# Four-layer hybrid attention network: both pairs of maxima of a step side by side, the second pair in a double bank, and each gated output split once

## The chip, the cores and the metric

The kernel runs on one core of one Trainium2 chip. The metric is the device time of one execution in microseconds (us). The engines are TensorE (PE, matrix products; PEld is its weight load), VectorE (DVE), ScalarE (ACT), GpSimd (POOL) and SyncE (SP, which only issues DMA here). A 128x512 float32 PSUM tile is one bank; PSUM holds eight.

## The reference

```python
for i in range(DEPTH):                       # 4 layers, mixer kinds A, B, C, A
    h  = rms_norm(x,  norm_g[i]) * (1 + sc)  + sh     # 1024 latent tokens, width 1024
    hc = rms_norm(xc, norm_g[i]) * (1 + scc) + shc    # 256 context tokens
    u, z = split(h @ w_in)                   # mixer columns and the gate
    o = mixer(u, uc, ...)                    # A: softmax(q k / 8) v, 16 heads, 4 kv heads
    x  = x  + gt  * ((o  * silu(z))  @ w_out)
    xc = xc + gtc * ((oc * silu(zc)) @ w_out)         # not in the last layer
return x
```

`sh`, `sc`, `gt` come from a product of the conditioning vector with `ada_w`. Mixer A attends from every token to context and latent keys; B within a window of 8 x 16; C takes the difference of two softmaxes.

## The kernel before, in words

Every product is done on float32 operands split in two parts, a rounded one (`hi`, made by `round_pool` on POOL, L130) and the rest (`lo`, by `sub` on DVE, L133); a product is three matmuls. The layers follow one another: projection of the norm's result, the z (gate) projection, attention, output projection.

**Attention A** (layers 0 and 3) works in units: a pair of heads by 512 queries, with ten key tiles in layer 0's latent part. `unit_events` gives each piece of a unit a time on a scale of steps and sorts them; one step holds two key tiles. In a step PE does the scores of two key tiles (`st`, L700 and L701, eight matmuls into two tiles from the pool `pa`, two buffers of two banks each), which ACT turns into exponentials (L705); the product of an earlier step's exponentials with the values (`o`, L725, eight matmuls, "PV"); and, for a unit ahead, two pairs of products (`sl` L653, `sc` L668) for the maximum over the keys, in single banks from the pool `pb` (four buffers). Each of these banks is reduced by one TENSOR_REDUCE on DVE (L660, L674). The times of the two pairs within a step are the table `SLOTS` (L781); scores stand at 0.05 and 0.15, PV at 0.4 and 0.45. The maxima of a unit become a row (`rows`: transpose `mT` L686, copy on ACT `mr` L688, a DMA), which takes part in the scores. The exponentials are summed on POOL and, for the last two key tiles, on DVE (L739), then `mixed` (L745, L747), a row sum on PE (L753) and the division. Only PE's order is pinned to the table's order; the other engines take theirs from the scheduler.

**out_proj** (from L872) runs over `work`, first all token tiles with the first half of the output columns (h=0), then all with the second (h=1): ten tiles, eight in the last layer. `start(i)` splits the gated output of the next tile into `ogt` hi and lo in two slots (four roundings on POOL, four subtractions on DVE); `products` makes 24 matmuls `y` (L897); DVE scales by the gate (`yg`, L934), POOL adds the residual (`xo`, L935). In h=1, except in the last layer, the tile's norm for the next layer follows: square sum, `rstd` on POOL, `xn` on DVE (L285), and one tile later eight transposes on PE (`xT`, L293) and the modulation (`hs`, ACT L314 and DVE L305; `hhi` L130, `hlo` L133). The slots come from one pool of 42 buffers of 128x1024 (`WHOLES`), which also holds the gated outputs, the probabilities and weights.

Of the kernel before, what the change touches and what calls it, by code (L numbers as in the profile page):

```python
# [15 lines left out]
ALU = mybir.AluOpType  # L16
AX = mybir.AxisListType
# [3 lines left out]
P = 128  # L21
D = 1024
KT = D // P
# [49 lines left out]
class Net:  # L73
# [554 lines left out]
    def softmax_unit(self, qscr, heads, Ks, vsrc, og, pair, t0, n, kts, finish):  # L628
# [19 lines left out]
        def max_lat(qt, c):  # L648

            for hh in range(2):  # L650
                k, q = high(hh, 0)
                ps = self.pb("sl")
                nc.tensor.matmul(  # L653
                    ps, q[:, qt * P : (qt + 1) * P], k[:, c * 512 : c * 512 + 512], start=True, stop=True,
                    tile_position=(hh * HD, 0),
                )
                st["ps", hh] = ps
            for hh in range(2):
                o = st["M"][:, hh * nq + qt, c : c + 1]
                nc.vector.tensor_reduce(out=o, in_=st["ps", hh], axis=AX.X, op=ALU.max)  # L660

        def max_ctx(a):
            ps = [self.pb("sc").rearrange("p (q k) -> p q k", k=CTX) for _ in range(2)]
            for i in range(2):
                qt = a * 2 + i
                for hh in range(2):
                    k, q = high(hh, 1)
                    nc.tensor.matmul(  # L668
                        ps[hh][:, i, :], q[:, qt * P : (qt + 1) * P], k, start=True, stop=True,
                        tile_position=(hh * HD, 0),  # L670
                    )
            for hh in range(2):
                o = st["M"][:, hh * nq + a * 2 : hh * nq + a * 2 + 2, 2 if lat else 0]
                nc.vector.tensor_reduce(out=o, in_=ps[hh], axis=AX.X, op=ALU.max)  # L674
# [34 lines left out]
        u.maxima = [lambda q=q, c=c: max_lat(q, c) for q in range(nq) for c in range(2) if lat]  # L709
        u.maxima += [lambda a=a: max_ctx(a) for a in range(nq // 2)]  # L710
# [70 lines left out]
    SLOTS = (0.25, 0.8)  # L781

    def unit_events(self, units, extra=()):
# [10 lines left out]
        for u, g in reversed(list(zip(units, starts))):  # L794
            if c >= g - self.LEAD:
                c, i = g - self.LEAD - 1, len(self.SLOTS) - 1
            for m in reversed(u.maxima):
                ev.append((c + self.SLOTS[i], m))
                c, i = (c, i - 1) if i else (c - 1, len(self.SLOTS) - 1)
# [61 lines left out]
    def out_proj(self, l, wop, steps, og, tiles):  # L861
# [46 lines left out]
        def start(i):  # L908
            ot = parts()
            split(work[i][1], range(4), ot)  # L910
            halves[i] = ot

        start(0)
        for i, (h, t) in enumerate(work):
# [9 lines left out]
            products(ps, h, halves.pop(i), range(KT))  # L924
# [793 lines left out]
```

## Time and profile before

| what | value |
|---|---|
| runs | 3665.51, 3666.45, 3667.39 us; median 3666.45 |
| profiled execution, its own time | 3671.03 us |
| its span; mean granted clock | 3669.2 us; 0.983 |
| PE / PEld busy | 3518.5 us (96%) / 2615.8 us (71%) |
| DVE / POOL / ACT busy | 2153.7 (59%) / 1998.8 (54%) / 1323.0 us (36%) |
| attention A, layer 0 (354 to 860 us) | PE 487.69 of 506, DVE 293.56, ACT 222.10, POOL 331.94 |
| attention A, layer 3 (3156 to 3560 us) | PE 399.26 of 404, DVE 253.78, ACT 187.45, POOL 308.20 |
| output projection, layer 0, h=0 (860 to 925 us) | PE 63.40 of 65 |
| splits of the gated output | POOL 304 x 0.57 us, DVE 304 x 0.56 us (173.3 and 170.8 us) |
| chain that ended last | PE 68%, DVE 16%, POOL 9% of the span |

The stages lie one behind the other, so each is read by itself: the busy time of each engine in its stretch, then what PE's idle time there waited for. In the timelines consecutive instructions of one kind are joined to one row (x8: eight of them), and the bracket tells how long the engine stood before the row and which instruction released it.

### The profile page before, as it was taken

What the parts mean: (1) busy time and instruction counts of PE and PEld (TensorE: products, weight loads), DVE (VectorE), ACT (ScalarE), POOL (GpSimd) and SP (SyncE); (2) the same over time, 40 slices, a digit from 0 to 9 for tenths busy, and PEclk for the clock granted to TensorE, in tenths of its full rate; (3) what the DMA queues carried; (4) which work ended last, traced back from release to release, by engine and by line L of the source; (5) the groups of instructions that cost most, each with busy time, mean ns of one, the idle gap of its engine ahead of it and who ended that gap; (6) DMA issues with size and microseconds to landing.
All of it is one profiled execution on the core that took longest, in us unless ns stands there. A gap on an engine that the chain in (4) does not pass through costs nothing.

```text
span 3669.2 us, 50527 instructions
## 1 busy us (share of the span) xinstructions
PE 3518.5 (96%) x18594; PEld 2615.8 (71%) x18594; DVE 2153.7 (59%) x3675; ACT 1323.0 (36%) x2756; POOL 1998.8 (54%) x2006
## 2 busy tenths in 40 slices
PE   7999999998899999999999999999989999999989
PEld 4887444446788888887778888888877787544447
DVE  5542555565742412888766510899995754566655
ACT  3221444441321212774222211677761221344430
POOL 5540656678631310667765510567776743477786
PEclk9999999999999999999999999999999999999989
DMA  6352543513244444552425432221313334111112
GB/s 208 78 135 83 158 130 103 182 55 97 96 116 138 104 126 111 166 151 69 138 78 137 130 117 61 82 87 38 98 40 99 110 93 125 46 46 37 46 39 86
DMA packets 229459, 370.39 MB, mean 101 GB/s; under 512 B 34088, under 2 KB 124120, under 8 KB 229212
## 3 DMA queue, kind: packets, MB, share of 16 engines
q1 hardware_dynamic: 228636, 367.01, 34.1%
q8 instruction: 148, 2.42, 0.3%
q14 instruction: 99, 0.81, 0.1%
q10 hardware_dynamic: 576, 0.15, 0.0%
HBM read 270.36 MB, written 96.57 MB: 100 GB/s over the span
## 4 chain that ended last, share of the span: by engine, by line
PE 68%; DVE 16%; POOL 9%; issue 4%; DMA 2%; ACT 1%; SPq 0%; POOLq 0%; ACTq 0%; DVEq 0%
PE proj L382 21%; PE zT L467 11%; PE o L725 8%; PE y L897 6%; PE st L700 5%; PE st L701 4%; PE sl L653 3%; DVE ml L1450 3%; PE o L1120 2%; POOL rstd L146 2%; DVE wlo L133 2%; DVE ogt L133 1%; PE qkT L437 1%; POOL hhi L130 1%; POOL p L739 1%
## 5 line engine op out<-in xcount | busy, mean ns | idle before, releaser
L739 POOL TENSOR_TENSOR p<-p,p 128x1024 f32<-128x1024 f32 x224 | 540.1, 2411 | 326.1 <-PE o L725 287.4
L382 PE MATMUL proj<-whi,hhi 128*128 128x512 f32 x1408 | 556.7, 395 | 3.2 <-POOL whi L130 1.9
L382 PE MATMUL proj<-wlo,hhi 128*128 128x512 f32 x1408 | 551.3, 392 | 3.9 <-DVE wlo L133 3.8
L382 PE MATMUL proj<-whi,hlo 128*128 128x512 f32 x1408 | 551.1, 391 | 0.0
L660 DVE TENSOR_REDUCE M<-sl 128x1 f32<-128x512 f32 x512 | 326.8, 685 | 292.5 <-PE sl L653 292.5
L705 ACT ACTIVATE p<-st 128x1024 f32<-128x1024 f32 (+1 forms) x336 | 324.4, 1003 | 314.8 <-PE st L701 303.1
L897 PE MATMUL y<-whi,ogt 128*128 128x512 f32 x1216 | 389.7, 398 | 16.7 <-POOL ogt L130 13.1
L133 DVE TENSOR_TENSOR wlo<-wraw,whi 128x1024 fp32r<-128x1024 f32 x136 | 213.5, 1584 | 217.8 <-POOL whi L130 193.0
L725 PE MATMUL o<-p,v 128*64 128x512 f32 x1344 | 324.5, 605 | 1.7 <-DVE M L660 1.1
L130 POOL TENSOR_SCALAR whi<-wraw 128x1024 fp32r<-128x1024 f32 x136 | 179.0, 1321 | 254.0 <-DMA wraw<-in_c_w_in_dram 91.3
L382 PEld LDWEIGHTS proj<-wlo,hhi 128*128 128x128 f32 x1408 | 265.8, 189 | 58.9 <-DVE wlo L133 6.0
L382 PEld LDWEIGHTS proj<-whi,hhi 128*128 128x128 f32 x1408 | 265.8, 189 | 57.5 <-POOL hhi L130 2.4
L382 PEld LDWEIGHTS proj<-whi,hlo 128*128 128x128 f32 x1408 | 265.6, 189 | 55.4
L897 PEld LDWEIGHTS y<-whi,ogt 128*128 128x128 f32 x1216 | 230.7, 190 | 73.2 <-POOL ogt L130 16.8
L467 PE MATMUL zT<-hhi,whi 128*128 128x512 f32 (+1 forms) x704 | 256.6, 365 | 5.9 <-DVE qklo L133 5.6
L404 ACT ACTIVATE y<-proj 128x1024 f32<-128x1024 f32 (+1 forms) x68 | 65.5, 964 | 527.4 <-PE proj L382 470.0
L467 PE MATMUL zT<-hhi,wlo 128*128 128x512 f32 (+1 forms) x704 | 254.3, 361 | 1.3 <-DVE wlo L133 1.3
L467 PE MATMUL zT<-hlo,whi 128*128 128x512 f32 (+1 forms) x704 | 254.2, 361 | 0.0
L897 PE MATMUL y<-wlo,ogt 128*128 128x512 f32 x608 | 239.6, 394 | 0.0
L146 POOL TENSOR_TENSOR rstd<-rstd,mhalf 128x16 f32<-128x16 f32 (+3 forms) x132 | 230.8, 1748 | 10.9
L700 PE MATMUL st<-q,k 128*128 128x512 f32 x512 | 218.3, 426 | 2.3 <-ACT p L705 2.3
L410 DVE TENSOR_TENSOR y<-y,rstd 128x1024 f32<-128x1024 f32 (+1 forms) x68 | 104.1, 1531 | 193.0 <-POOL rstd L146 193.0
(221 smaller groups left out, 7242.7 us busy)
## 6 DMA issues: line engine op xcount, KB each, us to landing
adaw<-in_ada_w_dram SPq DMA_DIRECT2D x96, 512.0 KB
xo<-xres SPq DMA_DIRECT2D x86, 256.0 KB
wraw<-in_a_w_in_dram SPq DMA_DIRECT2D x40, 512.0 KB
k<-k SPq DMA_DIRECT2D x40, 512.0 KB
q<-qkhi SPq DMA_DIRECT2D x76, 256.0 KB
q<-qklo SPq DMA_DIRECT2D x76, 256.0 KB
q<-q SPq DMA_DIRECT2D x136, 128.0 KB
wraw<-in_b_w_in_dram SPq DMA_DIRECT2D x32, 512.0 KB
```

Source lines behind the costliest of these rows:

```text
L130: self.nc.gpsimd.tensor_scalar(out=out, in0=in_, scalar1=1.0, scalar2=0.0, op0=ALU.mult, op1=ALU.add)
L133: self.nc.vector.tensor_tensor(out, a, b, op=ALU.subtract)
L146: nc.gpsimd.tensor_tensor(r, r, self.mhalf[:, :n], op=ALU.pow)
L382: nc.tensor.matmul(ps[:, i, :], self.h_op(a, 2 * tp + i, k), wop(b, k), start=(k == 0 and j == 0), stop=(k == KT - 1 and j == 2),)
L467: nc.tensor.matmul(ps, wop(a, k)[:, b * P : (b + 1) * P], self.h_cols(c, g, k), start=(k == 0 and j == 0), stop=(k == KT - 1 and j == 2),)
L660: nc.vector.tensor_reduce(out=o, in_=st["ps", hh], axis=AX.X, op=ALU.max)
L700: nc.tensor.matmul(ps[:, hh, :], self.k_op(K, 0, kt), q1[:, hh, :], start=True, stop=False)
L701: nc.tensor.matmul(ps[:, hh, :], self.k_op(K, 1, kt)[0 : HD + 1], q2[:, hh, :], start=False, stop=True)
L705: nc.scalar.activation(p, ps, AF.Exp, scale=HD**-0.5)
L725: nc.tensor.matmul(st["o"][hh * HD : (hh + 1) * HD, :], v(hh, kt), p[:, hh, :], start=j == 0, stop=j == N - 1, tile_position=(0, hh * HD),)
L739: eng.tensor_tensor(a, a, p, op=ALU.add)
L897: nc.tensor.matmul(ps, ot[a][:, k, :], wop[h](b, k), start=(k == 0 and j == 0), stop=(k == KT - 1 and j == 2))
```

## The change

The title given with the change names three things. The diff has lines for two of them; those of the differential layer (L1450, L1451) are the same in both programs.

1. `SLOTS` goes from (0.25, 0.8) to (0.25, 0.3), so the second pair of maxima of a step stands directly behind the first, ahead of PV. The second pair of a step (`i == 1`) goes into one tile of `pa` (two banks) and is reduced by one TENSOR_REDUCE over both (L658 of the changed file); the first stays in two tiles of `pb` (L661).
2. `start` in `out_proj` splits a token tile once, in h=0, and keeps the two slots until h=1 has used them.

```diff
--- before.py
+++ after.py
@@ -645,33 +645,47 @@
             K = st["K"][hh][kt][1 - hh] if kt == 0 else st["K"][hh][1][:, 1 - hh, :]
             return K[rows], st["q"][0][rows, hh, :]
 
-        def max_lat(qt, c):
-
+        def banks(double):
+
+            if double:
+                both = self.pa("sl")
+                return both, [both[:, hh * 512 : hh * 512 + 512] for hh in range(2)]
+            return None, [self.pb("sl") for _ in range(2)]
+
+        def largest(out, both, ps, n):
+
+            if both is not None:
+                nc.vector.tensor_reduce(out=out, in_=both.rearrange("p (h q k) -> p h q k", h=2, q=n), axis=AX.X, op=ALU.max)
+                return
+            for hh in range(2):
+                nc.vector.tensor_reduce(
+                    out=out[:, hh, :], in_=ps[hh].rearrange("p (q k) -> p q k", q=n), axis=AX.X, op=ALU.max
+                )
+
+        def max_lat(double, qt, c):
+
+            both, ps = banks(double)
             for hh in range(2):
                 k, q = high(hh, 0)
-                ps = self.pb("sl")
                 nc.tensor.matmul(
-                    ps, q[:, qt * P : (qt + 1) * P], k[:, c * 512 : c * 512 + 512], start=True, stop=True,
+                    ps[hh], q[:, qt * P : (qt + 1) * P], k[:, c * 512 : c * 512 + 512], start=True, stop=True,
                     tile_position=(hh * HD, 0),
                 )
-                st["ps", hh] = ps
-            for hh in range(2):
-                o = st["M"][:, hh * nq + qt, c : c + 1]
-                nc.vector.tensor_reduce(out=o, in_=st["ps", hh], axis=AX.X, op=ALU.max)
-
-        def max_ctx(a):
-            ps = [self.pb("sc").rearrange("p (q k) -> p q k", k=CTX) for _ in range(2)]
+            M = st["M"][:, : 2 * nq, c].rearrange("p (h q) -> p h q", h=2)
+            largest(M[:, :, qt : qt + 1], both, ps, 1)
+
+        def max_ctx(double, a):
+            both, ps = banks(double)
             for i in range(2):
                 qt = a * 2 + i
                 for hh in range(2):
                     k, q = high(hh, 1)
                     nc.tensor.matmul(
-                        ps[hh][:, i, :], q[:, qt * P : (qt + 1) * P], k, start=True, stop=True,
+                        ps[hh][:, i * CTX : (i + 1) * CTX], q[:, qt * P : (qt + 1) * P], k, start=True, stop=True,
                         tile_position=(hh * HD, 0),
                     )
-            for hh in range(2):
-                o = st["M"][:, hh * nq + a * 2 : hh * nq + a * 2 + 2, 2 if lat else 0]
-                nc.vector.tensor_reduce(out=o, in_=ps[hh], axis=AX.X, op=ALU.max)
+            M = st["M"][:, : 2 * nq, 2 if lat else 0].rearrange("p (h q) -> p h q", h=2)
+            largest(M[:, :, a * 2 : a * 2 + 2], both, ps, 2)
 
         def whole():
             st["mm"] = self.small([P, 32], "mm", 3)[:, : 2 * nq]
@@ -706,8 +720,8 @@
             st["p", j] = p
 
         u.load, u.whole, u.rows = load, whole, rows
-        u.maxima = [lambda q=q, c=c: max_lat(q, c) for q in range(nq) for c in range(2) if lat]
-        u.maxima += [lambda a=a: max_ctx(a) for a in range(nq // 2)]
+        u.maxima = [lambda d, q=q, c=c: max_lat(d, q, c) for q in range(nq) for c in range(2) if lat]
+        u.maxima += [lambda d, a=a: max_ctx(d, a) for a in range(nq // 2)]
         u.scores = [lambda j=j, kt=kt: scores(j, kt) for j, kt in enumerate(kts)]
         u.products, u.ends = finish(st, kts, n, pair, t0, og)
         return u
@@ -778,7 +792,7 @@
         return [lambda j=j, kt=kt: pv(j, kt) for j, kt in enumerate(kts)], ends
 
     LEAD = 2
-    SLOTS = (0.25, 0.8)
+    SLOTS = (0.25, 0.3)
 
     def unit_events(self, units, extra=()):
 
@@ -795,7 +809,7 @@
             if c >= g - self.LEAD:
                 c, i = g - self.LEAD - 1, len(self.SLOTS) - 1
             for m in reversed(u.maxima):
-                ev.append((c + self.SLOTS[i], m))
+                ev.append((c + self.SLOTS[i], lambda m=m, i=i: m(i == 1)))
                 c, i = (c, i - 1) if i else (c - 1, len(self.SLOTS) - 1)
             ev.append((min(c, g - self.LEAD - 6) - 1.5, u.load))
             n = len(u.scores) // 2
@@ -906,9 +920,11 @@
         halves = {}
 
         def start(i):
-            ot = parts()
-            split(work[i][1], range(4), ot)
-            halves[i] = ot
+
+            t = work[i][1]
+            if t not in halves:
+                halves[t] = parts()
+                split(t, range(4), halves[t])
 
         start(0)
         for i, (h, t) in enumerate(work):
@@ -921,7 +937,7 @@
                 ready.append(load(*work[i + 2]))
             full, x = ready.pop(0)
             ps = self.pb("y")
-            products(ps, h, halves.pop(i), range(KT))
+            products(ps, h, halves[t] if h == 0 else halves.pop(t), range(KT))
             while self.tail:
                 self.tail.pop(0)()
             if i + 1 == len(work) and not last:
```

PE, steady steps of attention A in layer 3: `st` scores, `sl` maxima, `o` PV. Before:

```order
L700 MATMUL st_5579_28616<-q1_5480_28245,k1_5483_28256 128x512
L701 MATMUL st_5579_28616<-q2_5481_28246,k2_5484_28257 128x512
L653 MATMUL sl_5581_28623<-k2_5484_28257,q1_5533_28445 128x512 [waits DVE_49]
L653 MATMUL sl_5582_28625<-k1_5483_28256,q1_5533_28445 128x512 [waits DVE_49]
L725 MATMUL o_5544_28479<-p_5570_28582,v_5195_26540 64x512 x2
L725 MATMUL o_5544_28479<-p_5572_28589,v_5195_26540 64x512 x2
L653 MATMUL sl_5586_28644<-k2_5484_28257,q1_5533_28445 128x512 [waits DVE_49]
L653 MATMUL sl_5587_28646<-k1_5483_28256,q1_5533_28445 128x512 [waits DVE_49]
L700 MATMUL st_5588_28650<-q1_5480_28245,k1_5483_28256 128x512 [waits Activation_49]
L701 MATMUL st_5588_28650<-q2_5481_28246,k2_5484_28257 128x512
```

Now (the same place, one step from its second score tile on):

```order
L714 MATMUL st_5452_28273<-q1_5367_27935,k1_5322_27756 128x512 [waits DVE_49]
L715 MATMUL st_5452_28273<-q2_5368_27936,k2_5323_27757 128x512
L714 MATMUL st_5452_28273<-q1_5367_27935,k1_5322_27756 128x512
L715 MATMUL st_5452_28273<-q2_5368_27936,k2_5323_27757 128x512
L670 MATMUL sl_5454_28280<-k2_5323_27757,q1_5412_28116 128x512
L670 MATMUL sl_5455_28281<-k1_5322_27756,q1_5412_28116 128x512
L670 MATMUL sl_5456_28286<-k2_5323_27757,q1_5412_28116 128x512 [waits Activation_49]
L670 MATMUL sl_5456_28286<-k1_5322_27756,q1_5412_28116 128x512
L739 MATMUL o_5422_28148<-p_5444_28241,v_5050_26070 64x512 x2
L739 MATMUL o_5422_28148<-p_5446_28248,v_5050_26070 64x512 x2
L714 MATMUL st_5460_28305<-q1_5367_27935,k1_5322_27756 128x512 [waits Activation_49]
L715 MATMUL st_5460_28305<-q2_5368_27936,k2_5323_27757 128x512
```

The second pair moved from behind the PVs to ahead of them; both of its matmuls write one tile, and the semaphores it waits for are ACT's, while the second score tile waits for DVE.

DVE, the h=1 pass of layer 0's output projection, one tile (`xn` norm, `ogt` split, `yg` gate, `hs` and `hlo` modulation). Before:

```order
L285 TENSOR_SCALAR xn_7112<-xo_6996,rstd_7116 128x1024 [waits DMAHW4_49,Pool_49]
L133 TENSOR_TENSOR ogt_7121<-og_617,ogt_7120 128x256 [waits Pool_49]
L133 TENSOR_TENSOR ogt_7121<-og_620,ogt_7120 128x256 [waits Pool_49]
L133 TENSOR_TENSOR ogt_7121<-og_622,ogt_7120 128x256 [waits Pool_49]
L133 TENSOR_TENSOR ogt_7121<-og_625,ogt_7120 128x256 [waits Pool_49]
L934 TENSOR_TENSOR yg_7193<-y_7133,gt_6603 128x512 [waits DMAHW7_49,PE_49]
L305 TENSOR_SCALAR hs_7168<-xT_7163,colA_589,colS_590 128x128 [waits PE_49]
L305 TENSOR_SCALAR hs_7168<-xT_7163,colA_589,colS_590 128x128 x3
L133 TENSOR_TENSOR hlo_7178<-hs_7168,hhi_7177 128x2x128 [waits Pool_49]
L133 TENSOR_TENSOR hlo_7182<-hs_7168,hhi_7181 128x2x128 [waits Pool_49]
L133 TENSOR_TENSOR hlo_7186<-hs_7168,hhi_7185 128x2x128 [waits Pool_49]
```

Now:

```order
L285 TENSOR_SCALAR xn_6997<-xo_6858,rstd_7001 128x1024 [waits DMAHW3_49,DMAHW0_49]
L950 TENSOR_TENSOR yg_7060<-y_7008,gt_6433 128x512 [waits PE_49]
L305 TENSOR_SCALAR hs_7043<-xT_7038,colA_589,colS_590 128x128 [waits PE_49]
L305 TENSOR_SCALAR hs_7043<-xT_7038,colA_589,colS_590 128x128 x3
L133 TENSOR_TENSOR hlo_6978<-hs_7043,hhi_6977 128x2x128 [waits Pool_49]
L133 TENSOR_TENSOR hlo_6982<-hs_7043,hhi_6981 128x2x128 [waits Pool_49]
L133 TENSOR_TENSOR hlo_6986<-hs_7043,hhi_6985 128x2x128 [waits DVE_49]
L133 TENSOR_TENSOR hlo_6990<-hs_7043,hhi_6989 128x2x128 [waits Pool_49]
L285 TENSOR_SCALAR xn_7064<-xo_6890,rstd_7068 128x1024 [waits DMAHW2_49,Pool_49]
L950 TENSOR_TENSOR yg_7127<-y_7075,gt_6433 128x512 [waits DMAHW5_49,PE_49]
```

Four subtractions that stood between `xn` and `yg` are gone from there.

POOL at the same place (`xo` residual). Before:

```order
L935 TENSOR_TENSOR xo_7080<-xo_7080,yg_7270 128x512 [waits DMAHW7_49,DVE_49]
L130 TENSOR_SCALAR hhi_7177<-hs_7253 128x2x128 [waits Activation_49]
L130 TENSOR_SCALAR hhi_7185<-hs_7253 128x2x128 [waits DVE_49]
L130 TENSOR_SCALAR hhi_7181<-hs_7253 128x2x128 [waits Activation_49]
L130 TENSOR_SCALAR hhi_7189<-hs_7253 128x2x128 [waits DVE_49]
L140 TENSOR_SCALAR rstd_7278<-ss_7276 128x1 [waits Activation_49]
L146 TENSOR_TENSOR rstd_7278<-rstd_7278,mhalf 128x1 [waits Pool_49]
L130 TENSOR_SCALAR ogt_7282<-og_618 128x256 [waits PE_49]
L130 TENSOR_SCALAR ogt_7282<-og_621 128x256
L130 TENSOR_SCALAR ogt_7282<-og_623 128x256
L130 TENSOR_SCALAR ogt_7282<-og_626 128x256
L935 TENSOR_TENSOR xo_7130<-xo_7130,yg_7347 128x512 [waits DMAHW5_49,DVE_49]
```

Now:

```order
L951 TENSOR_TENSOR xo_6930<-xo_6930,yg_7127 128x512 [waits DMAHW5_49,DVE_49]
L130 TENSOR_SCALAR hhi_6977<-hs_7110 128x2x128 [waits Activation_49]
L130 TENSOR_SCALAR hhi_6985<-hs_7110 128x2x128 [waits DVE_49]
L130 TENSOR_SCALAR hhi_6981<-hs_7110 128x2x128 [waits Activation_49]
L130 TENSOR_SCALAR hhi_6989<-hs_7110 128x2x128 [waits DVE_49]
L140 TENSOR_SCALAR rstd_7135<-ss_7133 128x1 [waits Activation_49]
L146 TENSOR_TENSOR rstd_7135<-rstd_7135,mhalf 128x1 [waits Pool_49]
L951 TENSOR_TENSOR xo_7005<-xo_7005,yg_7194 128x512 [waits DMAHW0_49,DVE_49]
```

The four roundings ahead of the next `xo` are gone.

## Rows read from the trace of the kernel before

**Rows 1.** Three h=1 passes: stretch, length, busy PE, PEld, DVE, ACT, POOL
```profile
925.00:1006.00 81.00, 70.12 (x339) 55.77 (x338) 65.94 (x126) 25.21 (x57) 61.10 (x100) 1.00 0.32 104
1780.00:1850.00 70.00, 61.26 (x291) 48.82 (x290) 61.17 (x117) 22.64 (x52) 56.00 (x93) 0.98 0.36 115
2830.00:2912.00 82.00, 71.67 (x339) 56.94 (x338) 66.19 (x126) 26.11 (x59) 63.34 (x102) 0.98 0.37 115
```

**Rows 2.** PE timeline, h=1, layer 0: start, duration, instruction, [idle before]
```profile
928.88 1.04 PE L293 MATMUL xT<-ident,xn 128*128 128x128 f32 x8
...
990.44 0.76 PE L293 MATMUL xT<-ident,xn 128*128 128x128 f32 x5 [0.96 <-DVE xn L285]
```

**Rows 3.** Timeline of DVE, layer 0's h=0 pass, two neighbouring tiles
```profile
907.32 0.69 DVE L934 TENSOR_TENSOR yg<-y,gt 128x512 f32<-128x512 f32 x1 [0.81 <-PE y L897]
912.76 0.69 DVE L934 TENSOR_TENSOR yg<-y,gt 128x512 f32<-128x512 f32 x1 [4.75 <-PE y L897]
```

**Rows 4.** Timeline of PE, one tile of layer 0's h=1 pass
```profile
944.14 1.09 PE L293 MATMUL xT<-ident,xn 128*128 128x128 f32 x8 [0.72 <-DVE xn L285]
944.99 0.48 PE L897 MATMUL y<-whi,ogt 128*128 128x512 f32 x1
...
951.63 1.09 PE L293 MATMUL xT<-ident,xn 128*128 128x128 f32 x8 [0.91 <-DVE xn L285]
```

**Rows 5.** Timeline of DVE, the same tile
```profile
944.01 2.01 DVE L133 TENSOR_TENSOR ogt<-og,ogt 128x256 fp32r<-128x256 f32 x4
945.94 0.68 DVE L934 TENSOR_TENSOR yg<-y,gt 128x512 f32<-128x512 f32 x1
...
950.68 0.89 DVE L285 TENSOR_SCALAR xn<-xo,rstd 128x1024 f32<-128x1024 f32 x1
```

**Rows 6.** Timeline of POOL, the same tile
```profile
946.70 1.29 POOL L935 TENSOR_TENSOR xo<-xo,yg 128x512 f32<-128x512 f32 x1 [1.29 <-DVE yg L934]
947.96 1.68 POOL L130 TENSOR_SCALAR hhi<-hs 128x256 fp32r<-128x256 f32 x4
```

**Rows 7.** Timeline of PE, a step of attention in layer 3
```profile
3254.73 0.50 PE L700 MATMUL st<-q,k 128*128 128x512 f32 x1
...
3256.80 0.51 PE L653 MATMUL sl<-k,q 64*128 64x512 f32 x2
3257.24 1.94 PE L725 MATMUL o<-p,v 128*64 128x512 f32 x8
3259.11 0.50 PE L653 MATMUL sl<-k,q 64*128 64x512 f32 x2
3259.54 0.50 PE L700 MATMUL st<-q,k 128*128 128x512 f32 x1
```

**Rows 8.** Timeline of PE, layer 0, two pairs of maxima side by side
```profile
359.92 0.73 PE L653 MATMUL sl<-k,q 64*128 64x512 f32 x4
360.59 0.50 PE L700 MATMUL st<-q,k 128*128 128x512 f32 x1
```

**Rows 9.** Timeline of ACT, the step of rows 7
```profile
3255.98 2.01 ACT L705 ACTIVATE p<-st 128x1024 f32<-128x1024 f32 x2 [2.79 <-PE st L701]
```

**Rows 10.** Timeline of PE, a step of layer 0 after a transposed row
```profile
370.19 0.50 PE L700 MATMUL st<-q,k 128*128 128x512 f32 x1
```

**Rows 11.** Timeline of ACT, the step of rows 10
```profile
372.48 0.27 ACT L688 ACTIVATE mr<-mT 8x128 fp32r<-8x128 f32 x1 [3.90 <-PE mT L686]
372.66 1.00 ACT L705 ACTIVATE p<-st 128x1024 f32<-128x1024 f32 x1
```

**Rows 12.** DVE's groups in layer C's attention: busy, mean ns, idle
```profile
L1450 DVE TENSOR_REDUCE ml<-st 128x1 f32<-128x1024 f32 x128 | 155.5, 1215 | 8.4 <-PE st L1383 8.3
```

**Rows 13.** Timeline of DVE, attention in layer 3, a unit's end
```profile
3407.83 1.29 DVE L660 TENSOR_REDUCE M<-sl 128x1 f32<-128x512 f32 x2 [1.21 <-PE sl L653]
3409.03 1.22 DVE L739 TENSOR_TENSOR p<-p,p 128x1024 f32<-128x1024 f32 x1
...
3410.77 1.22 DVE L747 TENSOR_TENSOR p<-p,p 128x1024 f32<-128x1024 f32 x1
```

## The prediction

> **What bounds the kernel now.** I read the page's shares first, then the busy time by stretch, then the list of PE's idle time by releaser, then the timelines of the two places that the diff touches. PE is busy 96% of the span (the table above) and nothing else is over 59%, so a saving must either be PE's own time or fill a gap that PE really has.
>
> Both exist. In the second half of the output projection (h=1) of layers 0 to 2, PE works 70.12 of 81, 61.26 of 70 and 71.67 of 82 us [rows 1]: 10.9, 8.7 and 10.3 us are unfilled, 30 together. The transposes of the next norm (L293) start at 928.88 and, eight tiles later, at 990.44 [rows 2]: 7.70 us a tile. A tile is 24 y matmuls and 8 transposes. In the first half (h=0), without transposes, tiles follow each other at 912.76 - 907.32 = 5.44 us [rows 3], and the transposes take 944.99 - 944.14 = 0.85 [rows 4]. PE could do a tile in 6.29. The rest is the wait that ends each time at DVE xn (0.72, 0.91 in [rows 4]).
>
> Why is xn late? On DVE four subtractions of ogt (2.01 us) stand between xn and yg, so yg begins at 945.94 [rows 5], although PE had finished the y it reads before the transposes at 944.14. From there the chain runs yg, POOL's xo at 946.70 after 1.29 idle "<-DVE yg", hhi at 947.96 [rows 6], the norm's rstd, xn at 950.68 [rows 5], xT at 951.63 [rows 4]: 5.69 us from yg to xT.
>
> In attention A (L0 and L3) PE is busy 487.7 of 506 and 399.3 of 404 us (the table), so only its own work can shrink. A steady step is scores at 3254.73, a pair of maxima at 3256.80, PV at 3257.24, the other pair at 3259.11, the next scores at 3259.54 [rows 7]: each lone pair holds PE for 0.43 to 0.44. Where by accident two pairs stand together (sl x4) they take 360.59 - 359.92 = 0.67 [rows 8], that is 0.23 for the second: 0.20 us less than a lone one.
>
> **Part 1: the split once.** 152 of 304 roundings on POOL and 152 of 304 subtractions on DVE go, 87 us of POOL (0.57 each, the table above) and 76 us of DVE (0.50 each by 2.01 for four [rows 5]). Almost all of it lies beside PE's matmuls and is worth nothing by itself. What counts is that in h=1 nothing of it stands ahead of yg any more (the DVE order above: xn, yg). Then yg starts when y ends, the chain of 5.69 follows, and xT is ready about 5.7 us after y's end; PE needs 0.85 + 5.44 = 6.29 for what stands in its queue until then. PE bounds, with 0.5 to spare. Gain: 7.70 - 6.29 = 1.41 a tile, 8 intervals a layer, 11.3; three layers would be 34 by that, and 30 by the unfilled time of [rows 1], which misses what a filled PE would also shift at the windows' edges. I take **31**. The last layer has no next norm, so its second half has no such wait: 0. In h=0 every split stays and is hidden as before. Bounds: at least 15, if after the cut the chain still misses PE by half the present wait (0.7 x 24 = 17, less a little for buffers), at most 34. The price of holding the halves is buffers: up to 20 of the 42 large slots stay taken through h=0, and are given back tile by tile in h=1, while the gated outputs are given back earlier, at the end of h=0. Nothing in the trace prices a wait for these slots; it would be a late first weight of the next layer. I take 0, since the two lists even out at the end of h=0 and h=1 frees two slots a tile, and as the bound 9 us: one tile's work of PE (6.29) waited out, half again, once.
>
> **Part 2: the maxima.** By the order of the changed program, 149 steps in the two attention stretches have both pairs together (76 in L0, 73 in L3). Gross: 149 x 0.20 = 30.
>
> The second pair now sits in a double bank of the pool in which the two score tiles also rotate: two buffers, three users. PE's order above shows its new waits: the second pair waits for the first exp (Activation), the next first score for the second exp, the next second score for DVE's double reduce.
> - *First exp.* The two exps together start 1.25 after the step's first score (3255.98 against 3254.73) and take 2.01, so the first ends at about +2.27 to +2.30 and its signal is there some 0.06 later (xn ends at 950.68 + 0.89 = 951.57, PE takes it at 951.63) [rows 4, 5, 7, 9]. PE wants the bank at 2.07 + 0.23 = +2.30. That is 0.03 to 0.09 of wait a step: the net is 0.14 a step, 149 x 0.14 = 21.
> - *Row copies.* In L0, six steps have the copy of the maxima's row (mr, L688) ahead of the exps in ACT's queue, and it waits for a transpose that stands behind all eight scores: scores at 370.19 [rows 10], exp only at 372.66, 2.47 later and not 1.25 [rows 11]. The second pair would stand 1 us there: 6 x 1.0 = -6. (Queued behind it on PE are the PVs and everything else.)
> - *Second exp.* It ends at +3.3, wanted at +4.66: no wait.
> - *Double reduce.* One reduce over 1024 columns of PSUM is 1.215 us in layer C [rows 12]; a pair of 512 is 1.29 [rows 13]. So DVE's work hardly changes. The first pair is done on PE at +2.6, its two reduces at +3.9, the double one at +5.05; the next second score wants the bank at 4.66 + 0.94 = +5.6. 0.5 to spare. Once in a unit of 5 steps DVE has also the last partial sums and the gate behind the reduces (3409.03 to 3411.99 [rows 13]); these move the double reduce of the next step to +10.4 on that scale (5.05 + 2.9, two reduces, the double one), and the score that wants its bank stands at 9.32 + 0.94 = +10.3 or, where the matmuls of the row sums come first, later. I put 2 us of loss to it: 30 such steps, at most 0.1 each.
> - Some 15 more adjacent pairs stand in the z projections: 15 x 0.14 = +2.
>
> Together 21 - 6 - 2 + 2 = **15**. Bounds: 30 (no wait at all) and 0 (each step waits what it saved); below that, the third rival.
>
> **Part 3.** The title's third part, the differential bias, has no lines in the diff; lines 1450 and 1451 stand in both. 0.
>
> Sum: 31 + 15 = 46. The profiled execution took 3671.0; 3625. It lies 4.6 above the median of the runs shown (3666.4), so the median to expect is **3620**.
>
> **Rivals.**
> 1. *The wait eats the switch.* Exp a lands 0.15 later than I reckon, each second pair waits what the missing switch saves. Part 2 gives 0, 31 remain: 3635. For it: the margin is 0.03 us, and it's read from a few steps. Against: ACT is busy 187 of 404 us, so nothing else holds the exps back in most steps.
> 2. *The norm's chain still bounds h=1* (hhi and the rstd queue on POOL behind xo; or the held slots stall a load). Part 1 gives 15 instead of 31, part 2 its 15: 3636; with rival 1 on top 3651. For it: the chain has only 0.5 us to spare. Against: what remains on POOL, four hhi and xo, is 3 us of 6.29.
> 3. *Slower: the double banks serialise.* If an addition on DVE (1.22 [rows 13]) stood ahead of the double reduce in every step, the next second score would wait 1.22 - 0.5 = 0.7 a step: 149 x (0.7 - 0.14) = 83 lost against 31 won, 3718. It decides once the reduce lands 0.85 us later than reckoned in all steps: 149 x (0.35 - 0.14) = 31. Against: the additions come once in five steps; there the loss would be 30 x 0.7 = 21 and the whole still 25 faster. The Trainium skill, Perfetto Trace Analysis, section Matmuls, speaks for this rival: independent matmul groups should rotate through different PSUM banks so that the evacuation of one overlaps the matmuls of the next. The change puts three groups on two double banks. By that rule the time would be this rival's; the kernel before keeps to the rule for its maxima, and no row shows three groups on two banks.
> 4. *Everything fits.* No wait in part 2 but the mr steps (30 - 6 + 2 = 26), 34 in part 1: 3606.
>
> **Chances.** Forecast 0.64 (3612 to 3630), rival 1 0.12, rival 2 0.11, rival 4 0.08, rival 3 0.05. A difference under 0.2% (7 us) can't be told from none. Faster 0.92: all but rival 3 and a bit of rival 2 at its worst with lost loads; same 0.03; slower 0.05. The range 3603 to 3650 leaves out rival 3 and some of the ends of 4 and 2.
>
> **What would show it.** Right: L293's starts in h=1 about 6.3 us apart, no idle "<-DVE xn"; in attention steps of about 4.66 instead of 4.80, with small idle "sl<-ACT p" and none at "st<-DVE M". Wrong: idle of PE at st with releaser DVE M (rival 3), sl<-ACT p of 0.2 a step (rival 1), xT still 7 us apart (rival 2), or first weights late at the start of projections.

## The result and the profile after

The changed kernel takes 3611.49 us (3609.91 to 3617.85, four runs) where the kernel before takes 3666.76 (3665.51 to 3667.39, four runs): a ratio of 0.9853, 95% interval 0.9836 to 0.987, 55 us less. The forecast was 46 less, 3620 in a range of 3603 to 3650. The profiled execution took 3609.91 us with a span of 3608.1 and a mean granted clock of 0.985. PE is busy 3471.8 us (96%), DVE 2057.5 (57%), POOL 1915.1 (53%): 46.7 us less work for PE, of which the maxima are the larger part, and 14.4 less idle time.

Where it went, by stages. A stage runs from its first matmul of the kind to the first of the next (from the timelines of PE; the projections hold the z projection and, in layers 0 and 3, the first maxima); e1 and e2 are the two parts of the change alone, explained below.

| stage, us | before | after | e1, split only | e2, maxima only |
|---|---|---|---|---|
| projections of layer 0 | 320.9 | 318.3 | 320.4 | 318.3 |
| attention A, layer 0 | 502.1 | 486.8 | 495.8 | 486.8 |
| output projections, layers 0, 1, 2 | 131.3, 130.0, 130.7 | 122.1, 119.8, 121.2 | 122.8, 119.7, 119.7 | 131.8, 129.3, 129.3 |
| attention, layers 1 and 2 | 263.9, 459.5 | 264.0, 459.4 | 264.0, 463.1 | 265.2, 458.9 |
| projections of layer 3 | 261.4 | 259.9 | 261.2 | 258.5 |
| attention A, layer 3 | 410.9 | 399.4 | 409.5 | 402.5 |

The output projections give 28.9 together and attention A with its z projections 31. In the profiled execution of before, the granted clock was 0.95 between 600 and 700 us, where e1, with the same code there, had 1.00 and got 473 matmuls done for 449 in the same 97.1 us of busy time. That made its layer 0 some 6 us longer. The fairer figure for attention A is against e1: 9.0 in layer 0 and 10.1 in layer 3, 19 together, and 3.4 with it in the two z projections.

**Output projection.** PE's transposes in the h=1 pass of layer 0, answering [rows 2, 4]:

```profile
911.28 1.03 PE L293 MATMUL xT<-ident,xn 128*128 128x128 f32 x8
...
917.65 1.03 PE L293 MATMUL xT<-ident,xn 128*128 128x128 f32 x8
...
949.35 1.03 PE L293 MATMUL xT<-ident,xn 128*128 128x128 f32 x8
...
957.02 1.10 PE L293 MATMUL xT<-ident,xn 128*128 128x128 f32 x8 [1.15 <-DVE xn L285]
...
963.44 1.03 PE L293 MATMUL xT<-ident,xn 128*128 128x128 f32 x8
```

They start 6.33 to 6.42 us apart, against 7.70 in the mean before, and have no idle before them. The exception is one tile a layer, the eighth: it starts 7.67 behind the seventh, 1.15 of it a wait for xn. So the eight intervals take 963.44 - 911.28 = 52.16 us instead of 61.56, 6.52 in the mean: 9.4 less a layer, 28 in three. DVE and POOL for one of these tiles, answering [rows 5, 6]:

```profile
928.95 0.75 DVE L285 TENSOR_SCALAR xn<-xo,rstd 128x1024 f32<-128x1024 f32 x1
930.52 0.69 DVE L950 TENSOR_TENSOR yg<-y,gt 128x512 f32<-128x512 f32 x1 [0.82 <-PE y L911]
...
935.27 0.75 DVE L285 TENSOR_SCALAR xn<-xo,rstd 128x1024 f32<-128x1024 f32 x1
```

```profile
931.29 1.29 POOL L951 TENSOR_TENSOR xo<-xo,yg 128x512 f32<-128x512 f32 x1 [2.38 <-DVE yg L950]
932.54 1.68 POOL L130 TENSOR_SCALAR hhi<-hs 128x256 fp32r<-128x256 f32 x4
```

yg now waits for y and not y for it: DVE stands 0.82 before it. From yg at 930.52 to xn's end at 936.02 the chain takes 5.5.

**Attention.** A steady step in layer 3 on PE, ACT and DVE, answering [rows 7, 9, 13]:

```profile
3229.03 0.50 PE L714 MATMUL st<-q,k 128*128 128x512 f32 x1
...
3231.09 0.76 PE L670 MATMUL sl<-k,q 64*128 64x512 f32 x4
3231.77 1.94 PE L739 MATMUL o<-p,v 128*64 128x512 f32 x8
3233.64 0.50 PE L714 MATMUL st<-q,k 128*128 128x512 f32 x1
```

```profile
3230.26 2.01 ACT L719 ACTIVATE p<-st 128x1024 f32<-128x1024 f32 x2 [2.60 <-PE st L715]
```

```profile
3231.61 1.29 DVE L661 TENSOR_REDUCE M<-sl 128x1 f32<-128x512 f32 x2 [2.19 <-PE sl L670]
3232.82 1.21 DVE L658 TENSOR_REDUCE M<-sl 128x2 f32<-128x1024 f32 x1
```

The four maxima products take 0.68, as in [rows 8], and the step 3233.64 - 3229.03 = 4.61 instead of 4.80. The exps start 1.23 into the step. The reduces start at +2.58, and the double one is done at +5.0, as worked out. Taken apart, the second pair of the four and the first of the two exps are:

```profile
3231.42 0.43 PE L670 MATMUL sl<-k,q 64*128 64x512 f32 x2
```

```profile
3230.26 1.03 ACT L719 ACTIVATE p<-st 128x1024 f32<-128x1024 f32 x1 [2.60 <-PE st L715]
```

The pair starts 0.33 behind the first pair (3231.42 against 3231.09), at +2.39; the exp whose bank it takes has ended at +2.26.

PE's idle time at the scores and maxima, first in layer 0 (355 to 842 us), then in layer 3 (3108 to 3508 us); columns as in [rows 12]:

```profile
L714 PE MATMUL st<-q,k 128*128 128x512 f32 x256 | 108.7, 425 | 2.6 <-ACT p L719 1.6 <-DVE M L658 0.9
...
L670 PE MATMUL sl<-k,q 64*128 64x512 f32 x236 | 48.5, 464 | 6.9 <-ACT p L719 6.5
```

```profile
L714 PE MATMUL st<-q,k 128*128 128x512 f32 x256 | 109.1, 426 | 7.9 <-DVE M L658 6.4 <-ACT p L719 1.6
...
L670 PE MATMUL sl<-k,q 64*128 64x512 f32 x232 | 44.6, 462 | 0.0
```

In the kernel before, the wait for DVE in layer 3 stood at the maxima (3156 to 3560 us):

```profile
L653 PE MATMUL sl<-k,q 64*128 64x512 f32 x235 | 60.8, 502 | 3.5 <-DVE M L660 3.3
```

The waits after the change are these: 6.5 us at the maxima for ACT in layer 0, none in layer 3, and 6.4 at the scores for DVE's reduce in layer 3. Of the 6.4, 4.87 are one wait, which stood in the kernel before as one of 3.33, and 1.5 lie in the first two steps of the stretch.

### The profile page after: what moved, and what is told of

Read it like the earlier page. It is cut to its first block, busy times and chain, and to the rows that moved or that the text cites. A ratio compares the mean times of both kernels' runs of the same rounds, so it can differ in the third digit from the quotient of the medians.

```text
span 3608.1 us, 49956 instructions
## 1 busy us (share of the span) xinstructions
PE 3471.8 (96%) x18594; PEld 2608.3 (72%) x18594; DVE 2057.5 (57%) x3358; ACT 1320.9 (37%) x2756; POOL 1915.1 (53%) x1854
## 4 chain that ended last, share of the span: by engine, by line
PE 73%; DVE 14%; POOL 7%; issue 3%; ACT 1%; DMA 1%; SPq 0%; POOLq 0%; ACTq 0%; DVEq 0%
PE proj L382 22%; PE zT L467 11%; PE y L911 9%; PE o L739 7%; PE st L714 4%; PE st L715 4%; DVE ml L1466 3%; PE sl L670 2%; PE o L1136 2%; POOL p L753 2%; DVE wlo L133 1%; PE qkT L437 1%; POOL rstd L146 1%; PE ada L195 1%; PE pT L1214 1%
## 5 line engine op out<-in xcount | busy, mean ns | idle before, releaser
L661 DVE TENSOR_REDUCE M<-sl 128x1 f32<-128x512 f32 (+1 forms) x326 | 209.8, 685 | 293.2 <-PE sl L670 243.5
L658 DVE TENSOR_REDUCE M<-sl 128x2 f32<-128x1024 f32 (+1 forms) x165 | 200.6, 1216 | 45.2 <-PE sl L670 40.1
```

The source lines that it names most:

```text
L658: nc.vector.tensor_reduce(out=out, in_=both.rearrange("p (h q k) -> p h q k", h=2, q=n), axis=AX.X, op=ALU.max)
L661: nc.vector.tensor_reduce(out=out[:, hh, :], in_=ps[hh].rearrange("p (q k) -> p q k", q=n), axis=AX.X, op=ALU.max)
```

## The experiments

**e1 and e2: the two parts apart.** e1 is the kernel before with the new `start` and `products` call of the diff, e2 the changed kernel with the old ones.

> Only the split of the gated output is made once; the maxima stay as before. Theory (the subtractions of ogt ahead of yg made the norm's chain late, in the h=1 passes of three layers): 28 to 31 us faster than before (ratio 0.9915 to 0.9924), the whole gain in the three output projections, each 9 to 10 us shorter (131 to 122), and attention within 2 us of before. Rival (the two parts help each other, or part of the gain in the projections comes from the maxima): under 20 us faster.

> Only the maxima are changed (adjacent pairs, second in a double bank); the split is made twice as before. Theory (one change between kinds of product less per step, 0.18 to 0.19 us in 149 steps and some in the z projections): 26 to 31 us faster than before, steps of 4.62 instead of 4.80, output projections as before. The forecast's own term would give 15. Rival: the profiled pair of runs overstates it, 15 to 20.

Measured: e1 3635.26, ratio 0.9909 (0.9893 to 0.9926), 31.7 us faster than the 3666.99 of before; e2 3642.07, ratio 0.9927 (0.9913 to 0.9942), 24.9 faster. Together 56.6, the whole of the change's 55.3. The table shows that each acts in its own stages alone: in e1 the output projections shrink to 120 to 123 and not the attention beyond before's clock, in e2 the reverse (e1's layer 2 is 3.6 longer, though no line of the change touches it). The gains add, so the parts are independent as far as these runs can tell. The first part of the forecast (31) stands; the second is worth 25, or 24 as the difference of the change and e1, and not 15. e2 came out just short of what I then expected from the profiled pair (26 to 31), since that pair's before had lost 6 us to its clock.

**e3: adjacent, but in single banks.** The kernel before with one line changed:

```diff
-    SLOTS = (0.25, 0.8)
+    SLOTS = (0.25, 0.3)
```

> Before with the second pair of maxima moved next to the first, all four in single banks, two reduces each, no double bank. Theory (adjacency needs the double bank: the four single banks also hold PV's sum, so the fourth product waits for the first reduce, which ends about 1.2 us later): each of 149 steps some 0.8 to 1.1 us longer than in the changed kernel, 90 to 130 us slower than before, PE idle at sl with DVE M as releaser. Rival (single banks come free in time): the same 4.62 a step, 26 to 31 faster than before.

Measured: 3757.66, ratio 1.0246 (1.0231 to 1.0261), 91 us slower than before. PE in its attention of layer 3:

```profile
L725 PE MATMUL o<-p,v 128*64 128x512 f32 x626 | 153.5, 611 | 8.1 <-DVE M L660 8.1
...
L653 PE MATMUL sl<-k,q 64*128 64x512 f32 x240 | 63.1, 471 | 30.0 <-DVE M L660 29.9
```

Its steady step is 5.63 us, 1.02 more than in the changed kernel, and the releaser of the idle time is the reduce of a maximum. The theory holds: to put the pairs side by side without the second double bank costs much more than the switch it saves.

**e4: the double bank, but apart.** The changed kernel with the slots of before:

```diff
-    SLOTS = (0.25, 0.3)
+    SLOTS = (0.25, 0.8)
```

> The changed kernel with the second pair of a step back behind PV (slot 0.8), still in the double bank and reduced at once. Split made once. Theory (the double bank only comes free in time because the pair stands early): the pair ends at about +4.9 of the step, its reduce at +6.15, the second score wants the bank at 4.80 + 0.94 = +5.74, so 0.4 of wait in each of 149 steps, 60 lost: 25 to 35 us slower than before in spite of the split's 29. Rival (the double bank costs nothing anywhere): 28 to 31 us faster than before, steps of 4.80.

Measured: 3746.14, ratio 1.0213 (1.0198 to 1.0228), 79 us slower than before, worse than expected. PE at the scores of layer 3:

```profile
L714 PE MATMUL st<-q,k 128*128 128x512 f32 x256 | 115.8, 452 | 33.9 <-DVE M L658 19.6 <-ACT p L719 14.2
```

Half of it is the wait foreseen, for DVE's double reduce. The other half, 14.2 us for ACT, I had left out: the second score comes late, so the second exp does, and the next step's tile waits for that one. A step takes 5.26. Every fifth one takes 7.0 to 9.5 (5.5 in the changed kernel): there DVE does three operations for the end of a unit ahead of the double reduce, and PE waits for it:

```profile
3236.05 0.50 PE L714 MATMUL st<-q,k 128*128 128x512 f32 x1 [1.93 <-DVE M L658]
```

This is the third rival of the prediction, made to happen: with three users of two double banks, the place of the second pair in the step decides between 4.61 and 5.26. The Trainium skill, Perfetto Trace Analysis, section Matmuls (independent matmul groups should rotate through different banks so that evacuation overlaps), is borne out here, while in the changed kernel, with the same banks, the order alone leaves the steady step free of such waits.

**e5: the first pair in the double bank.** This tests the margin at the first exp.

```diff
-                ev.append((c + self.SLOTS[i], lambda m=m, i=i: m(i == 1)))
+                ev.append((c + self.SLOTS[i], lambda m=m, i=i: m(i == 0)))
```

> The changed kernel with the double bank given to the first pair of a step instead of the second; adjacency, reduces and split as in the change. Theory (the pair in the double bank waits for the first exp, which ends 2.3 us into the step, and the second pair stands just there): the first pair, wanted at +2.07, waits about 0.28 a step, some 149 x 0.26 = 39 us slower than the changed kernel, 3645 to 3655, PE idle at sl with ACT p as releaser of 30 to 45 us. Rival (the margin at the exp is wider than the rows suggest): 3610 to 3620, as the changed kernel.

Measured: 3627.33, ratio 0.9886 (0.9871 to 0.99), some 12 us slower than the changed kernel by the ratios, 16 by the medians. The steady step is as expected, 4.85, with the maxima at +2.33 and 0.19 of idle ahead of them "<-ACT p": the first exp releases the bank 0.26 after the place of the first pair, while the second pair stands 0.33 behind that place and so finds it free in the changed kernel. But the whole is less than half of what 149 such steps would cost: the stages are 494.2 in layer 0, 7 more than in the changed kernel, and 413.1 in layer 3, 14 more, where 76 and 73 steps would give 17 each. By PE's timelines, 62 of the 87 steps of layer 0 are longer, by 13.9 in all, and 70 of the 79 of layer 3 by 15.9. Back come 6.7 and 2.2, for the most part in the steps where the changed kernel stands for ACT's copies of rows, at the start of the stretch, and at the wait of 4.87 us below. The steps with a row's transpose lose less (4.86 against 4.69 in layer 0).

**e6: the row's transpose behind the maxima.**

```diff
-            ev.append((g - self.LEAD + 0.17, u.rows))
+            ev.append((g - self.LEAD + 0.35, u.rows))
```

> The changed kernel with the transpose of the maxima's row (mT) behind both pairs of the step instead of ahead of them, so that ACT's copy of the row no longer stands ahead of the exps. Theory (the 6.5 us of PE idle at sl behind ACT p in layer 0 come from these copies): idle there under 2, time 3 to 6 us shorter than the changed kernel, 3605 to 3609. Rival (the row then comes late for its scores): PE idle at the scores, time as the changed kernel or longer.

Measured: 3610.26, ratio 0.9837 (0.9822 to 0.9851). PE at the maxima of layer 0:

```profile
L670 PE MATMUL sl<-k,q 64*128 64x512 f32 x236 | 47.6, 464 | 2.4 <-ACT p L719 2.3
```

The idle for ACT goes from 6.5 to 2.3, where under 2 was expected, and the stage from 486.8 to 482.0. So most of these waits were the row copies. In the total it is 6 us by the ratios and 1 by the medians, inside the scatter; the stage shows it, the total does not settle it.

**e7 and e8: which half of the split made the chain late.** In h=1, e7 makes the low half again, e8 the high half; the other is kept.

```diff
             if t not in halves:
                 halves[t] = parts()
                 split(t, range(4), halves[t])
+            else:
+                again(t, range(4), halves[t])
```

```python
def again(t, blocks, ot):                 # e7; e8: ot[0] and round_pool instead
    g, o = t // 4, (t % 4) * P
    ot[1] = self.slot([P, KT, P], F32R, "ogt")
    for b in blocks:
        a = og.block(b, g)[:, :, o : o + P]
        hi, lo = (x[:, 2 * b : 2 * b + 2, :] for x in ot)
        self.sub(lo, a, hi)
```

> The changed kernel, but in h=1 the low halves are made anew (152 subtractions on DVE back, ahead of yg as before), the high halves kept. Theory (DVE's subtractions ahead of yg made the chain late): most of the split's gain is lost, output projections of three layers back to 129 to 131 us, 25 to 30 slower than the changed kernel, 3636 to 3641. Rival (POOL's roundings made it late, the subtractions only waited for them): output projections stay near 121, 3611 to 3618.

> The changed kernel, but in h=1 the high halves are made anew (152 roundings on POOL back, ahead of xo as before), the low halves kept. Theory (subtractions on DVE are the cause; the roundings end about 2 us after y's end at the latest, and delay xo by 1.2 of which the chain has 0.5 to spare): 10 to 17 us slower than the changed kernel, 3621 to 3628. Rival (only POOL matters): 3636 to 3641; (POOL does not matter at all): 3611 to 3614.

Measured: e7 3627.94, ratio 0.9885 (0.987 to 0.99); e8 3618.76, ratio 0.9861 (0.9845 to 0.9878). The output projections are 125.8, 123.6, 123.6 in e7 and 122.9, 120.6, 120.5 in e8. PE in e7 and DVE ahead of one of its tiles:

```profile
936.50 1.09 PE L293 MATMUL xT<-ident,xn 128*128 128x128 f32 x8 [0.19 <-DVE xn L285]
...
943.25 1.09 PE L293 MATMUL xT<-ident,xn 128*128 128x128 f32 x8 [0.19 <-DVE xn L285]
```

```profile
935.69 0.75 DVE L285 TENSOR_SCALAR xn<-xo,rstd 128x1024 f32<-128x1024 f32 x1
936.36 1.42 DVE L133 TENSOR_TENSOR ogt<-og,ogt 128x256 fp32r<-128x256 f32 x4
937.70 0.68 DVE L961 TENSOR_TENSOR yg<-y,gt 128x512 f32<-128x512 f32 x1
```

PE in e8 and POOL ahead of the same tile:

```profile
930.48 1.03 PE L293 MATMUL xT<-ident,xn 128*128 128x128 f32 x8
...
936.82 1.03 PE L293 MATMUL xT<-ident,xn 128*128 128x128 f32 x8
```

```profile
929.07 1.95 POOL L130 TENSOR_SCALAR ogt<-og 128x256 fp32r<-128x256 f32 x4
931.46 1.29 POOL L961 TENSOR_TENSOR xo<-xo,yg 128x512 f32<-128x512 f32 x1 [0.44 <-DVE yg L960]
```

Both expectations were too high. With the subtractions alone the tile shown takes 6.75, PE waits 0.19 for xn (the eight intervals are 6.99 in the mean), and 10 of the split's 29 us are lost in these stages (12 by the ratios). With the roundings alone it takes 6.34: the stages lose 1 us (the ratios differ by 3, inside the scatter), since the four end 0.44 before xo can start. That leaves more than half which only the two together cost: four subtractions are 1.42 us when POOL makes no roundings, 2.01 beside them [rows 5], and xn 0.75 against 0.89. These two, 0.59 and 0.14, are 0.73 of the 0.74 by which the tile of [rows 4], 951.63 - 944.14 = 7.49, is longer than this one in e7.

**e9 and e10: the third part of the title.** No line of the diff touches the differential layer. There one DVE operation scales the first maximum, and a second joins it with the other one; one can do both:

```diff
-                nc.vector.tensor_scalar_mul(mx, mx, -SC)
...
-                nc.vector.scalar_tensor_tensor(
-                    out=mx[:, m : m + 1], in0=ml, scalar=-SC, in1=mx[:, m : m + 1], op0=ALU.mult, op1=ALU.min
-                )
+                nc.vector.tensor_scalar(
+                    out=mx[:, m : m + 1], in0=ml, scalar1=mx[:, m : m + 1], scalar2=-SC, op0=ALU.max, op1=ALU.mult
+                )
```

e10 adds e6's edit to it.

> The changed kernel, and in the differential layer the maximum and the scale in one operation: the scaling of the first maximum (64 operations of 128x2, 31 us of DVE) goes, and the later step takes the larger of the two and scales it. This is what the third part of the title could mean. Theory (DVE is busy 420 of 459 us in that layer and its chain runs through the maxima): 5 to 20 us faster than the changed kernel, all of it in the differential layer. Rival (the operation stands in time in which DVE waits for PE's scores): within 3 us of the changed kernel.

> The changed kernel with both edits, the row's transpose behind the maxima and the one operation in the differential layer. If the two gains stand in different layers they add: about 4 us from the first, and what the run with the second alone shows; a total under the changed kernel's by 4 to 24 us. Rival: no further gain, 3608 to 3612.

Measured: e9 3590.72, ratio 0.9789 (0.9775 to 0.9804), 21 us under the changed kernel; e10 3585.56, ratio 0.9774 (0.9758 to 0.9791), 26 under it; both a little beyond what was expected. The differential attention went from 459.4 to 436.6 us. Its stretch and PE's wait at the context scores, in the changed kernel:

```profile
2268.00:2727.00 459.00, 422.57 (x2925) 379.79 (x2923) 422.08 (x852) 332.41 (x953) 317.16 (x443) 0.95 0.22 65
```

```profile
L1398 PE MATMUL sc<-kc,q 128*128 128x256 f32 x127 | 40.1, 334 | 21.7 <-ACT pc L1478 21.7
```

In e9:

```profile
2269.00:2705.00 436.00, 411.30 (x2922) 370.33 (x2920) 400.11 (x788) 333.10 (x953) 315.36 (x443) 0.97 0.23 68
```

```profile
L1398 PE MATMUL sc<-kc,q 128*128 128x256 f32 x126 | 38.8, 328 | 11.0 <-ACT pc L1477 11.0
```

DVE's busy time fell by 22 and the stretch by as much; PE's idle at the context scores for ACT's exps, which need the maximum, was halved, 11 us. The other half is PE's own time, 411.30 us busy for 422.57 on the same work, with a granted clock of 0.97 for 0.95. So DVE's queue set a part of the pace there, and that the shorter waits also brought the higher clock is likely, not shown.

**e11: the stall in layer 3.** In the changed kernel one wait of 4.87 us stands alone. DVE, POOL and PE there, and the stretches around it:

```profile
3446.72 3.37 DVE L133 TENSOR_TENSOR wlo<-wraw,whi 128x1024 fp32r<-128x1024 f32 x1 [4.52 <-POOL whi L130]
3450.01 1.28 DVE L661 TENSOR_REDUCE M<-sl 128x1 f32<-128x512 f32 x2
```

```profile
3445.64 1.04 POOL L130 TENSOR_SCALAR whi<-wraw 128x1024 fp32r<-128x1024 f32 x1
3446.65 5.63 POOL L753 TENSOR_TENSOR p<-p,p 128x1024 f32<-128x1024 f32 x2
```

```profile
3443.84 0.75 PE L670 MATMUL sl<-k,q 64*128 64x512 f32 x4
...
3452.48 0.80 PE L714 MATMUL st<-q,k 128*128 128x512 f32 x1 [4.87 <-DVE M L658]
3453.07 0.63 PE L715 MATMUL st<-q,k 65*128 65x512 f32 x1
3453.50 0.63 PE L714 MATMUL st<-q,k 128*128 128x512 f32 x1
```

```profile
3440.00:3446.00 6.00, 6.00 (x28) 2.67 (x28) 2.20 (x3) 2.46 (x4) 5.84 (x5) 1.00 0.02 5
3446.00:3453.00 7.00, 2.13 (x9) 1.18 (x6) 5.70 (x4) 1.02 (x1) 6.92 (x4) 0.78 0.00 0
3453.00:3458.00 5.00, 5.00 (x16) 1.83 (x14) 2.68 (x4) 1.02 (x1) 0.30 (x1) 0.62 0.00 0
3458.00:3463.00 5.00, 5.00 (x26) 2.58 (x24) 4.97 (x6) 1.95 (x2) 0.97 (x1) 1.00 0.00 0
```

DVE stands at a subtraction of a weight (wlo), whose rounding POOL finishes at 3446.68; it runs beside POOL's additions for 3.37 us (the shortest of its kind in the kernel before is 1.21), and the maxima of 3443.84 are reduced only behind it. PE waits, and when it starts again at 3452.48 its products are 0.43 apart where they were 0.23: the granted clock is 0.62 over 3453 to 3458, so part of it was at the level of 1.2 GHz, and 1.00 again, 2.4 GHz, from 3458. The step takes 11.65 us: 4.61 as the others, 4.87 of waiting, and some 2.2 for the lower clock. e11 is e10 with the roundings some steps earlier:

```diff
-            extra = [(0.0, 0.8, early), (0.75, 0.92, loads), (0.83, 1.0, highs), (0.85, 1.02, lows)]
+            extra = [(0.0, 0.8, early), (0.75, 0.92, loads), (0.81, 0.97, highs), (0.85, 1.02, lows)]
```

> The kernel with both further edits, and the roundings of the output weights during attention some steps earlier (0.81 to 0.97 of the layer instead of 0.83 to 1.0), the subtractions where they were. Theory (the 4.87 us of PE idle in layer 3 and the clock's fall behind it come from one subtraction that stands on DVE ahead of the maxima's reduces and waits there for its rounding): that idle falls under 2 us, time 3 to 10 us shorter than with the two edits alone, 3576 to 3583. Rival (the subtraction itself, 3.4 us beside POOL's additions, is enough): idle and time within 3 us of the run with the two edits.

Measured: 3574.55, ratio 0.9748 (0.973 to 0.9766), the fastest of all, 11 us under e10 (9.5 by the ratios), at the far end of what was expected. PE at the scores in layer 3:

```profile
L714 PE MATMUL st<-q,k 128*128 128x512 f32 x255 | 108.6, 426 | 1.1 <-DVE M L658 0.6 <-ACT p L719 0.4
```

The idle for DVE's reduce is 0.6. Attention A of layer 3 takes 394.7, against 407.6 in e10, 399.4 in the changed kernel and 402.5 to 402.8 in e2, e6, e7, e8 and e9. The subtraction now waits for nothing, but it also lies beside other work of POOL and takes 2.13 instead of 3.37, so the run alone doesn't part its wait from its length. The rows above do, as an estimate: with DVE's queue done 4.52 earlier, 0.35 of the 4.87 would be left.

## Why the prediction was right, point by point

- **Where the gain lies**: right. Both stages were the ones with a gap or with PE's own time to shrink, and apart from the z projections no other stage moved by more than 0.7 us.
- **The split, 31**: e1 measured 31.7, 28 of it by the tiles of h=1 and 30 by the three stages. Most tiles take 6.34 where the working had 6.29, but with the eighth the mean is 6.52: the gain is 1.18 a tile and not 1.41. The working's own product, 34, was not reached; the 31 chosen between it and the unfilled 30 fits better than the step it came from. The mechanism was named too narrowly: it put the delay down to four subtractions standing ahead of yg for 2 us. e7 shows that they alone cost 0.47 of the 1.18 a tile, e8 that the roundings alone cost 0.10. The delay needs both, because each DVE operation is longer beside POOL's.
- **Held buffers, 0**: right. The first weights of the next layers came no later; the projections of layers 1 and 2 are 458.6 and 461.4 us, 458.8 and 461.8 before.
- **The maxima, 15**: mis-sized, 24 to 25. The step that failed is "0.03 to 0.09 of wait a step: the net is 0.14". It took the 0.23 that a second pair costs PE for the distance at which that pair starts. It starts 0.33 behind the first, at +2.39 and not +2.30, when the first exp's bank is free; PE's idle at the maxima of layer 3 is 0.0 and a step is 0.19 shorter: 149 x 0.19 = 28. The rest of the working held: the row copies cost 6.5 us of waiting in layer 0 (6 forecast), DVE arriving late cost about 3 us more than before, at three places of layer 3 and not in thirty steps (3.3 of idle at the maxima there before, 6.4 at the scores now), and the z projections of layers 0 and 3 give 2.1 and 1.3 (against e1). That is 22 of the 24 to 25. How near the wait at the first exp lies is what e5 shows, where the pair that needs the bank stands 0.33 earlier and waits 0.19 a step.
- **Double reduce done at +5.05**: +5.0 in the trace.
- **Rival 1** (the wait eats the switch) didn't come: its margin was wider. **Rival 2** (the chain still bounds h=1): only at one tile a layer, the eighth, 7.67 behind the seventh, where POOL does rstd, waiting for ACT, ahead of hhi; these are 1.33 a layer, 4 in all. **Rival 3** (the double banks serialise) didn't come in this order, and is real: e4 gives it, at 0.65 a step and some 1.5 to 4 us in every fifth. **Rival 4**, nothing waits, was nearer than the forecast by its size for the maxima (26).
- **Part 3, 0**: right for this diff, as the layer's 459.4 us show. The operation that the title speaks of was still there to be had, 21 us (e9).

## What to carry to other kernels

To save a change between kinds of matmul, look first for the place where each buffer comes free: a step with the same two pairs costs 4.61 us, 5.26 or 5.63 by the order of two items and the kind of bank. An operation that repeats what another pass made is worth cutting where it stands ahead of the chain that PE waits for, and its price there isn't its busy time but what the engines beside it lose as well. An operation that waits in a queue for another engine's result blocks all that stands behind it; ask for its input earlier before you make it shorter.

## What the runs showed that I had not expected

- DVE and POOL slow each other on these tiles. Four subtractions of 128x256 take 1.42 us alone (e7), 2.01 beside roundings [rows 5]. In e8 one of the four roundings is longer too, 0.84 beside xn where the others take 0.40. On large tiles one can see how: the subtraction of 128x1024 at 3446.72 starts 0.07 behind an addition on POOL, and the next addition stands behind both:

```profile
3446.65 2.35 POOL L753 TENSOR_TENSOR p<-p,p 128x1024 f32<-128x1024 f32 x1
```

```profile
3449.08 3.20 POOL L753 TENSOR_TENSOR p<-p,p 128x1024 f32<-128x1024 f32 x1
```

  The subtraction ends at 3450.09, 1.09 after the first addition's end, and alone it takes 1.21; the second addition takes 0.85 more than the first. So each stood for the other. The Trainium skill, SBUF — State Buffer, section Who interferes with whom, says that a DVE instruction with two SBUF inputs contends with a GpSimd instruction that reads SBUF, and that what they contend for is an exclusive lock. The trace agrees here, 3.37 for 1.21.
- A wait of 4.87 us costs more than itself: over the 5 us from 3453 on, PE's granted clock was 0.62, some 2.2 us lost.
